# The recurrent gates as tanh of half the argument, in three rounded passes, with two steps of the recurrence on another engine

## The chip, the cores and the metric

The kernel runs on one core of a Trainium2 chip. The metric is the device time of one execution in microseconds (us). Five engines work at once, each through its own instructions in order: TensorE (PE, matmuls; PEld is its weight loading), VectorE (DVE), ScalarE (ACT), GpSimd (POOL) and SyncE (SP, which issues most DMAs). They wait for each other through semaphores only. All data is float32. An "fp32r" tile holds float32 numbers that were rounded, so that TensorE takes them in one pass.

## The reference, cut to what matters

Two transformer blocks run one after the other on 512 tokens of width 1024. The first (token mixer with a gated delta rule, then a mixture of 32 experts) is not touched by the change. The second has 16 meta tokens ahead of the 512, so T = 528. It runs attention and a two-way linear recurrence side by side, merges them and ends with a feed-forward layer. The change lies in the recurrence:

```python
xc = centred_dwconv(xr, conv_w[l], conv_b[l])            # 4 taps, xr = part of xn @ w_in
...
def rg_lru(xc, wa, ba, wx, bx, lam, reverse):            # once forward, once reverse
    xb = xf.reshape(B, T, RNN_BLOCKS, RNN_BLOCK)         # 8 blocks of 128 channels
    r = jax.nn.sigmoid(jnp.einsum('btnc,ncd->btnd', xb, wa) + ba)
    i = jax.nn.sigmoid(jnp.einsum('btnc,ncd->btnd', xb, wx) + bx)
    log_a = RG_C * r * jax.nn.log_sigmoid(lam)
    a = jnp.exp(log_a)
    u = jnp.sqrt(-jnp.expm1(2.0 * log_a)) * (i * xf)
    _, h = lax.associative_scan(_linear_recurrence_combine, (a, u), axis=1, reverse=reverse)
...
rnn = (forward + reverse) * jax.nn.gelu(gr)
mix = g_attn * attn + g_rnn * rnn
```

## The kernel before

The program is one straight stream per engine. The second block's mixing stage goes in eight rounds, n = 0 to 7: round n handles attention head n and recurrence block n, each 128 channels on the partitions and the tokens along the free axis. The order on PE is written out by hand (`manual_schedule` in `block2`); the order on the other engines is set by a scheduler when the program is built, except that ACT's table functions keep the order of the code (`act`). PSUM tiles come from three pools of two buffers each: `psA` and `psB` of one bank, `psD` of two banks. A tile is written again only when the reader of its old contents is done.

What PE does in a middle round, in its order, with the names used below:

- the gates (L2027): 2 directions x 2 gates, each one `psD` tile of two halves of 264 tokens; plain float32 matmuls of the weights `wg` with the convolved input `xc`. ACT empties each tile through a sigmoid into `rg` or `ig`.
- the scores of attention head n, token tiles 0 and 1, into `psD` (`weights`, through `mm3`, L198 to L200: high part, low part, high part again).
- two dense products (`dense_fm`, 24 passes of 512 columns each), the transposes of the first two score tiles between them, then the scores of token tiles 2 and 3.
- `rnn_x` of block n+1: a dense product of 2 x 24 passes of 264 columns into `psA`; ACT copies it to `xr`, DVE runs the four taps (L2007, L2009) into `xc`.
- the transposes of the last two score tiles, which ACT and DVE split into `PThi` and `PTlo`.
- the first dense product of round n+1, then the product of head n's weights with its values (`psB`, from `PThi` and `PTlo`), then the gates of round n+1. In round 7 two of the four gate tiles stand ahead of this product.

Behind the gates runs `rnn` for block n-1, without PE: tanh, exp and square on ACT, a product on DVE, two square roots on ACT (`th`), the products L2079 and one scan for each direction on DVE (L2082), their sum (L2084) and the product with the gate (L2085). `rn[n]` then goes into the mix (`ao`, L2144), which ACT and DVE split for the output product (`ga`, `rn`). Sigmoid, exp with tanh, and the square root lie in three different tables of ACT; every change between them is an ACT_TABLE_LOAD.

`split` is one ACT copy to the high part (L90) and one DVE subtraction for the low part (L170), so L90 and L170 stand for nearly all ACT work and all such subtractions.

Of the kernel before, what the change touches and what calls it, by code (L numbers as in the profile page):

```python
# [9 lines left out]
FT = mybir.dt.float32  # L10
FR = mybir.dt.float32r
I32 = mybir.dt.int32
BF = mybir.dt.bfloat16
AF = mybir.ActivationFunctionType
OP = mybir.AluOpType
# [18 lines left out]
META = 16  # L34
# [19 lines left out]
def halves(x):  # L54

    return x.rearrange("p (s c) -> p s c", s=2)


def by_turns(x):

    return x.rearrange("p (s c) -> p c s", s=2)


def unturned(x):

    return x.rearrange("p (c s) -> p s c", s=2)
# [9 lines left out]
class Net:  # L76
# [1893 lines left out]
    def rnn_start(self, p, vec):  # L1970

        nc = self.nc
        x = vec[:, 72:88]
        cl = p.tile([128, 2, 16], FT, name="cl")
        y = p.tile([128, 16], FT, name="cl_y")
        c = cl[:, 0, :]
        nc.vector.scalar_tensor_tensor(y, x, -1.0, x, op0=OP.mult, op1=OP.min)
        self.act(y, y, AF.Exp)
        self.log1p_unit(p, c, y, 16)
        nc.vector.tensor_scalar(y, x, 0.0, None, op0=OP.min)  # L1980
        nc.vector.tensor_tensor(c, y, c, OP.subtract)
        nc.vector.tensor_scalar(c, c, 8.0, None, op0=OP.mult)
        nc.vector.tensor_scalar(cl[:, 1, :], c, -1.0, None, op0=OP.mult)
        return cl

    def rnn_x(self, p, n, vec, xT):

        nc, I = self.nc, self.I
        T = META + S
        H = T // 2  # L1990
        nhi, nlo = xT
        wg = p.tile([128, 2, 2, 128], FT, name="wg")
        nc.sync.dma_start(wg[:, 0], I["rg_wa_2"][0, :, n].rearrange("d c e -> c d e"))
        nc.sync.dma_start(wg[:, 1], I["rg_wx_2"][0, :, n].rearrange("d c e -> c d e"))
        hi, lo = self.wchunk(I["w_in_2"][0], 0, NK, 1536 + n * 128, 128)
        xr = p.tile([128, T + 3], FT, name="xr")
        nc.vector.memset(xr[:, 0:2], 0.0)
        nc.vector.memset(xr[:, T + 2:], 0.0)
        for j in range(2):
            js = slice(j * H, (j + 1) * H)  # L2000
            ps = self.psA.tile([128, 512], FT, name="psA")
            for k in range(NK):
                self.mm3(ps[:, :H], hi[:, k, :], lo[:, k, :], by_turns(nhi[:, k, js]), by_turns(nlo[:, k, js]),
                         k == 0, k == NK - 1)
            self.act(halves(xr[:, 2 + j * H:2 + (j + 1) * H]), unturned(ps[:, :H]), AF.Copy)
        c = p.tile([128, T], FT, name="xc")
        nc.vector.tensor_scalar(c, xr[:, 0:T], vec[:, n:n + 1], vec[:, 32 + n:33 + n], op0=OP.mult, op1=OP.add)  # L2007
        for j in range(1, 4):
            nc.vector.scalar_tensor_tensor(c, xr[:, j:j + T], vec[:, 8 * j + n:8 * j + n + 1], c,  # L2009
                                           op0=OP.mult, op1=OP.add)  # L2010
        return c, wg

    def rnn_gates(self, p, n, vec, x, meanwhile=lambda: None):

        nc = self.nc
        T = META + S
        H = T // 2
        c, wg = x
        rg = p.tile([128, 2, T], FT, name="rg")
        ig = p.tile([128, 2, T], FT, name="ig")  # L2020
        for d in range(2):
            if d:
                meanwhile()
            for w, dst, bias in ((0, rg, 40), (1, ig, 56)):
                ps = self.psD.tile([128, 2, 512], FT, name="psD")
                for j in range(2):
                    nc.tensor.matmul(ps[:, j, :H], wg[:, w, d, :], c[:, j * H:(j + 1) * H], start=True, stop=True)  # L2027
                self.act(dst[:, d, :].rearrange("p (a b) -> p a b", a=2), ps[:, :, :H], AF.Sigmoid,
                         bias=vec[:, bias + 8 * d + n:bias + 8 * d + n + 1])
        nc.vector.tensor_tensor(ig, ig, c[:, None, :].to_broadcast([128, 2, T]), OP.mult)  # L2030
        return rg, ig

    def gates(self, p, n, xT, rn, ga):
# [25 lines left out]
    def rnn(self, p, n, cl, st, rn):  # L2059

        nc = self.nc
        T = META + S
        rg, ig = st
        u = p.tile([128, 2, T], FT, name="th", bufs=1)
        for d in range(2):
            q = 8 * d + n
            r, t = rg[:, d, :], u[:, d, :]
            self.act(t, r, AF.Tanh, scale=cl[:, 1, q:q + 1])
            self.act(r, r, AF.Exp, scale=cl[:, 0, q:q + 1])

            a2 = p.tile([128, T], FT, name="a2", bufs=1)
            self.act(a2, r, AF.Square)
            nc.vector.scalar_tensor_tensor(t, a2, 1.0, t, op0=OP.add, op1=OP.mult)
        yield
        for d in range(2):
            self.act(u[:, d, :], u[:, d, :], AF.Sqrt, scale=0.0625)
        for d in range(2):
            t, g, r = u[:, d, :], ig[:, d, :], rg[:, d, :]
            nc.vector.tensor_tensor(g, g, t, OP.mult)  # L2079
            if d:  # L2080
                t, g, r = t[:, ::-1], g[:, ::-1], r[:, ::-1]
            nc.vector.tensor_tensor_scan(t, r, g, 0.0, op0=OP.mult, op1=OP.add)  # L2082
        f = u[:, 0, META:]
        nc.vector.tensor_tensor(f, f, u[:, 1, META:], OP.add)  # L2084
        nc.vector.tensor_tensor(rn[n], rn[n], f, OP.mult)  # L2085
        yield

    def attention(self, tp, h, kv, rn, ga, gp, mix):
# [225 lines left out]
```

## Time and profile before

| | |
|---|---|
| time, median of 3 runs | 1925.61 us (1924.58 to 1929.8) |
| the profiled execution | 1932.37 us, span 1930.6 us |
| PE busy in the span | 1802.8 us (93%) |
| DVE, ACT, POOL busy | 987.3, 708.0, 31.1 us |
| the stretch of the eight rounds | about 1246 to 1563 us of the span |
| one middle round (gates to gates) | 34.70 us |

The profiled execution is the one the rows come from; it took 6.8 us longer than the median. The profile lists each instruction's start, its duration, and, in square brackets, the engine's idle time before it with what ended that. A PE row's duration contains the time that the pipeline takes to empty, so that rows overlap; how fast PE really goes is read from the distance between starts.

### The profile page before, as it was taken

The numbers are of one execution on the slowest core, as the hardware profiler recorded it, in microseconds if no ns is written. First come the engines' busy times: TensorE is split into PE (matmuls) and PEld (weight loads), VectorE is DVE, ScalarE is ACT, GpSimd is POOL, SyncE is SP. The second block draws the span as 40 slices with busy tenths as digits, with TensorE's granted clock in tenths as the row PEclk, the third lists the DMA queues.
The fourth block names the chain that finished last, engine by engine and source line by source line (L and its number), as shares of the span: only waits on it lengthen the run. The fifth ranks groups of instructions, "written<-read, shape, count | busy, mean of one in ns | idle before, by whom it ended". The sixth has DMA issues, their size and how long they took to land. (4 is left out here: it accounts for less than half of the span.)

```text
span 1930.6 us, 23857 instructions
## 1 busy us (share of the span) xinstructions
PE 1802.8 (93%) x9285; PEld 1357.0 (70%) x9285; DVE 987.3 (51%) x1843; ACT 708.0 (37%) x1157; POOL 31.1 (2%) x39
## 2 busy tenths in 40 slices
PE   6999999989999699988988968999999989999999
PEld 5887888868898534433333326888888778888887
DVE  6853787735555603222121249567877863333333
ACT  5333544424323311111010116457777733332332
POOL 0000000000000000000000000000000000000000
PEclk9999999989999799999999998999999999999999
DMA  8655766876286599999999873332222233333332
GB/s 256 98 121 94 126 88 88 152 173 97 77 298 260 223 425 424 425 426 425 425 425 426 369 274 134 115 109 67 71 77 66 87 100 104 104 98 102 103 123 66
DMA packets 252133, 372.65 MB, mean 193 GB/s; under 512 B 30386, under 2 KB 192723, under 8 KB 228083
## 3 DMA queue, kind: packets, MB, share of 16 engines
q1 hardware_dynamic: 241218, 342.79, 55.9%
q10 hardware_dynamic: 7632, 16.78, 2.3%
q0 software_dynamic: 3168, 11.54, 1.5%
q8 instruction: 74, 1.21, 0.3%
q14 instruction: 41, 0.33, 0.1%
HBM read 349.03 MB, written 22.04 MB: 192 GB/s over the span
## 5 line engine op out<-in xcount | busy, mean ns | idle before, releaser
L90 ACT ACTIVATE whi<-raw 128x1024 fp32r<-128x1024 f32 (+1 forms) x203 | 234.0, 1157 | 426.5 <-PE psA L199 267.2
L170 DVE TENSOR_TENSOR wlo<-raw,whi 128x1024 fp32r<-128x1024 f32 (+1 forms) x195 | 249.4, 1280 | 244.0 <-ACT whi L90 233.4
L1271 PE MATMUL psB<-mwt,XT 128*64 128x512 f32 x1008 | 234.2, 600 | 13.7 <-ACT XT L90 8.9
L1271 PEld LDWEIGHTS psB<-mwt,XT 128*64 128x64 f32 x1008 | 74.0, 138 | 161.4 <-issue 137.5
L200 PE MATMUL psA<-hT_hi,wlo 128*128 128x512 f32 (+1 forms) x456 | 176.4, 387 | 9.3 <-DVE wlo L170 9.3
L199 PE MATMUL psA<-hT_lo,whi 128*128 128x512 f32 (+1 forms) x456 | 177.6, 389 | 0.0
L198 PE MATMUL psA<-hT_hi,whi 128*128 128x512 f32 (+1 forms) x456 | 176.3, 387 | 0.9 <-ACT whi L90 0.9
L1304 PE MATMUL psB<-mwt,hbT 128*64 128x512 f32 x480 | 119.1, 604 | 23.1 <-DMA mwt<-in_w 21.8
L1336 DVE TENSOR_TENSOR res<-res,psA 128x512 f32<-128x512 f32 x128 | 79.4, 681 | 118.1 <-PE psA L1331 118.1
L199 PE MATMUL psA<-hn_lo,whi 128*128 128x512 f32 (+1 forms) x368 | 136.3, 370 | 0.3 <-DVE hn_lo L2178 0.3
L198 PE MATMUL psA<-hn_hi,whi 128*128 128x512 f32 (+1 forms) x368 | 136.4, 371 | 0.2 <-ACT hn_hi L90 0.2
L200 PE MATMUL psA<-hn_hi,wlo 128*128 128x512 f32 (+1 forms) x368 | 136.2, 370 | 0.0
L1280 DVE TENSOR_TENSOR sl<-sl,psB 128x512 f32<-128x512 f32 x16 | 11.0, 688 | 203.2 <-PE psB L1271 203.2
L198 PE MATMUL psA<-xn_hi,whi 128*128 128x512 f32 (+1 forms) x320 | 109.4, 342 | 0.4 <-ACT qx L90 0.4
L200 PE MATMUL psA<-xn_hi,wlo 128*128 128x512 f32 (+1 forms) x320 | 108.2, 338 | 0.0
L199 PE MATMUL psA<-xn_lo,whi 128*128 128x512 f32 (+1 forms) x320 | 108.1, 338 | 0.0
L1304 PEld LDWEIGHTS psB<-mwt,hbT 128*64 128x64 f32 x480 | 37.7, 138 | 98.6 <-issue 57.5
L200 PEld LDWEIGHTS psA<-hT_hi,wlo 128*128 128x128 f32 (+1 forms) x456 | 86.3, 189 | 22.0 <-DVE wlo L170 10.3
L90 ACT ACTIVATE hbT<-psA 128x512 f32<-128x512 f32 x16 | 9.6, 597 | 240.9 <-PE psA L1288 240.9
L198 PEld LDWEIGHTS psA<-hT_hi,whi 128*128 128x128 f32 (+1 forms) x456 | 86.3, 189 | 13.6 <-ACT whi L90 1.3
L199 PEld LDWEIGHTS psA<-hT_lo,whi 128*128 128x128 f32 (+1 forms) x456 | 86.3, 189 | 12.0
L199 PEld LDWEIGHTS psA<-hn_lo,whi 128*128 128x128 f32 x368 | 69.5, 189 | 9.5 <-DVE hn_lo L2178 0.5
(567 smaller groups left out, 3487.7 us busy)
## 6 DMA issues: line engine op xcount, KB each, us to landing
mwt<-in_w SPq DMA_DIRECT2D x188, 1024.0 KB, 20.6
raw<-in_w_in SPq DMA_DIRECT2D x108, 512.0 KB, 6.8
raw<-in_w_ffn_in SPq DMA_DIRECT2D x44, 512.0 KB, 3.9
raw<-in_w_ffn_out SPq DMA_DIRECT2D x22, 512.0 KB, 3.6
raw<-in_w_pa SPq DMA_DIRECT2D x8, 512.0 KB, 4.4
raw<-in_w_pb SPq DMA_DIRECT2D x8, 512.0 KB, 5.5
raw<-in_w_o SPq DMA_DIRECT2D x8, 512.0 KB, 7.7
raw<-in_w_out SPq DMA_DIRECT2D x8, 512.0 KB, 3.7
```

Source lines behind the costliest of these rows:

```text
L90: ins = self.nc.scalar.activation(out, in_, func, **kw)
L170: return self.nc.vector.tensor_tensor(lo, x, hi.bitcast(FT), OP.subtract)
L198: nc.tensor.matmul(out, whi, xhi, start=first, stop=False)
L199: nc.tensor.matmul(out, whi, xlo, start=False, stop=False)
L200: nc.tensor.matmul(out, wlo, xhi, start=False, stop=last)
L1271: nc.tensor.matmul(ps[CAP * i:CAP * (i + 1), :], XT[:, r0 + k, CAP * i:CAP * (i + 1)], w_, start=(r0 + k == 0), stop=(r0 + k == NK - 1))
L1280: nc.vector.tensor_tensor(so, so, h[1], OP.mult)
L1304: nc.tensor.matmul(pys[half][CAP * i:CAP * (i + 1), :], hT[:, r0 + k, CAP * i:CAP * (i + 1)], ws[i][:, k, half * 512:(half + 1) * 512], st ...
L1336: nc.vector.tensor_tensor(x, x, unturned(ps), OP.add)
```

## The change

- Gate weights `wg` and the convolved input `xc` are split into high and low parts (`ws`, `cs`), and each gate half is made by `mm3`: three passes of rounded operands in place of one float32 matmul. The input is read "by turns" (first and second half of the columns alternating), and ACT's reading of the tile undoes this.
- The sigmoid becomes tanh of half the argument. What follows is adapted: biases times one half, `c` times 4 in place of 8, `scale` and `bias` both given to the tanh and exp of `rnn`, `ig` made by (tanh + 1) times `xc`, another scale in the root.
- Behind the two roots a tanh of one column (`warm`) is put, so that the table with exp and tanh is loaded there.
- The last two steps of the recurrence (sum of directions, product with the gate) go from DVE to POOL.
- Buffers: `wghi`, `xclo` and `xc` have one buffer, the low weights share the name `wg` and the high input the name `xr`, with two buffers each.

```diff
-        nc.vector.tensor_scalar(c, c, 8.0, None, op0=OP.mult)
+        nc.vector.tensor_scalar(c, c, 4.0, None, op0=OP.mult)
+
+        nc.vector.tensor_scalar(vec[:, 40:72], vec[:, 40:72], 0.5, None, op0=OP.mult)
...
+        ws = p.tile([128, 2, 2, 128], FR, name="wghi", bufs=1), p.tile([128, 2, 2, 128], FR, name="wg")
+        self.split(*ws, wg)
...
-        c = p.tile([128, T], FT, name="xc")
+        c = p.tile([128, T], FT, name="xc", bufs=1)
...
-        return c, wg
+        cs = p.tile([128, T + 3], FR, name="xr")[:, 0:T], p.tile([128, T], FR, name="xclo", bufs=1)
+        self.split(*cs, c)
+        return c, cs, ws
...
-                    nc.tensor.matmul(ps[:, j, :H], wg[:, w, d, :], c[:, j * H:(j + 1) * H], start=True, stop=True)
-                self.act(dst[:, d, :].rearrange("p (a b) -> p a b", a=2), ps[:, :, :H], AF.Sigmoid,
+                    js = slice(j * H, (j + 1) * H)
+                    self.mm3(ps[:, j, :H], whi[:, w, d, :], wlo[:, w, d, :], by_turns(chi[:, js]), by_turns(clo[:, js]),
+                             True, True)
+                self.act(dst[:, d, :].rearrange("p (a s c) -> p a s c", a=2, s=2),
+                         ps[:, :, :H].rearrange("p a (c s) -> p a s c", s=2), AF.Tanh, scale=0.5,
                          bias=vec[:, bias + 8 * d + n:bias + 8 * d + n + 1])
-        nc.vector.tensor_tensor(ig, ig, c[:, None, :].to_broadcast([128, 2, T]), OP.mult)
+        nc.vector.scalar_tensor_tensor(ig, ig, 1.0, c[:, None, :].to_broadcast([128, 2, T]), op0=OP.add, op1=OP.mult)
...
-            self.act(t, r, AF.Tanh, scale=cl[:, 1, q:q + 1])
-            self.act(r, r, AF.Exp, scale=cl[:, 0, q:q + 1])
+            self.act(t, r, AF.Tanh, scale=cl[:, 1, q:q + 1], bias=cl[:, 1, q:q + 1])
+            self.act(r, r, AF.Exp, scale=cl[:, 0, q:q + 1], bias=cl[:, 0, q:q + 1])
...
-            self.act(u[:, d, :], u[:, d, :], AF.Sqrt, scale=0.0625)
+            self.act(u[:, d, :], u[:, d, :], AF.Sqrt, scale=0.25 ** 3)
+
+        self.act(self.small.tile([128, 1], FT, name="warm"), cl[:, 0, 0:1], AF.Tanh)
...
-        nc.vector.tensor_tensor(f, f, u[:, 1, META:], OP.add)
-        nc.vector.tensor_tensor(rn[n], rn[n], f, OP.mult)
+        nc.gpsimd.tensor_tensor(f, f, u[:, 1, META:], OP.add)
+        nc.gpsimd.tensor_tensor(rn[n], rn[n], f, OP.mult)
```

Where the instructions stand changes with it. On DVE, before, in a middle round, from the products of the roots (`ig<-ig,th`) on; the scans print as SCALAR_TENSOR_TENSOR `th<-rg,ig`:

```order
L2079 TENSOR_TENSOR ig<-ig,th 128x528 x2
L2007 TENSOR_SCALAR xc<-xr,vec_5912 128x528
L170 TENSOR_TENSOR PTlo<-psD,PThi 16x128
L2009 SCALAR_TENSOR_TENSOR xc<-xr,vec_5912,xc 128x528
L170 TENSOR_TENSOR PTlo<-psD,PThi 16x128
L2009 SCALAR_TENSOR_TENSOR xc<-xr,vec_5912,xc 128x528
L170 TENSOR_TENSOR PTlo<-psB,PThi 128x4x128
L2009 SCALAR_TENSOR_TENSOR xc<-xr,vec_5912,xc 128x528
L170 TENSOR_TENSOR PTlo<-psB,PThi 128x4x128
L2082 SCALAR_TENSOR_TENSOR th<-rg,ig 128x528 x2
L170 TENSOR_TENSOR wlo<-raw,whi 128x1024
L2084 TENSOR_TENSOR th<-th 128x512
```

And on DVE after, from the same place of a middle round on:

```order
L2090 TENSOR_TENSOR ig<-ig,th 128x528 x2
L2093 SCALAR_TENSOR_TENSOR th<-rg,ig 128x528 x2
L2011 TENSOR_SCALAR xc<-xr,vec_5912 128x528
L170 TENSOR_TENSOR PTlo<-psD,PThi 16x128
L2013 SCALAR_TENSOR_TENSOR xc<-xr,vec_5912,xc 128x528
L170 TENSOR_TENSOR PTlo<-psD,PThi 16x128
L2013 SCALAR_TENSOR_TENSOR xc<-xr,vec_5912,xc 128x528
L170 TENSOR_TENSOR PTlo<-psB,PThi 128x4x128
L2013 SCALAR_TENSOR_TENSOR xc<-xr,vec_5912,xc 128x528
L170 TENSOR_TENSOR PTlo<-psB,PThi 128x4x128
L2155 TENSOR_TENSOR ao<-ao,rn_8975 128x512
L170 TENSOR_TENSOR xclo<-xc,xr 128x528
```

The two scans moved ahead of the taps and of the four `PTlo`; the POOL steps can run from the second scan on, and the mix and the low part of the gates' input (`xclo`) follow the last `PTlo`. In round 7 the rows there are the same.

On ACT, before, in a middle round, from the splits of the next weights to the copies out of the gate tiles (`ga_10460<-ao` is the high part of a finished mix, `ga_8967<-psA` a merge gate):

```order
L90 ACTIVATE whi<-raw 128x1024 x2
L90 ACT_TABLE_LOAD
L90 ACTIVATE rg<-psD,vec_5912 128x528
L90 ACTIVATE ig<-psD,vec_5912 128x528
L90 ACTIVATE ga_10460<-ao 128x512
L90 ACTIVATE rg<-psD,vec_5912 128x528
L90 ACTIVATE ig<-psD,vec_5912 128x528
L90 ACTIVATE ga_8967<-psA 128x512
L90 ACT_TABLE_LOAD
L90 ACTIVATE pr,s<-psD,m,qs 128x528 x2
```

And on ACT after, from the same place on:

```order
L90 ACTIVATE whi<-raw 128x1024
L90 ACTIVATE xr<-xc 128x528
L90 ACTIVATE whi<-raw 128x1024
L90 ACTIVATE ga_10587<-ao 128x512
L90 ACTIVATE rg<-psD,vec_5912 128x528
L90 ACTIVATE ig<-psD,vec_5912 128x528
L90 ACTIVATE rg<-psD,vec_5912 128x528
L90 ACTIVATE wghi<-wg 128x512
L90 ACTIVATE ig<-psD,vec_5912 128x528
L90 ACTIVATE ga_8968<-psA 128x512
```

Both table loads are gone from this stretch, the mix's high part moved ahead of the four gate copies, and the high part of the next round's gate weights (`wghi`) stands ahead of the fourth. The table with exp is loaded directly behind the roots instead. After the last round the root of the following norm (`mo_r`) has a table load ahead of it that it had not before.

## Rows read from the trace of the kernel before

**Rows 1.** The page's first line.

```profile
span 1930.6 us, 23857 instructions
```

**Rows 2.** The windows view, one stretch of 35 us: busy time of each engine.

```profile
1365.00:1400.00 35.00, 33.93 (x198) 29.44 (x197) 28.07 (x52) 25.85 (x45) 0.00 (x0) 1.00 0.27 78
```

**Rows 3.** Timeline of PE, one middle round: start, duration, line, tiles, count, idle before.

```profile
1398.51 3.89 PE L2027 MATMUL psD<-xc,wg 128*128 128x264 f32 x16
1403.37 0.38 PE L198 MATMUL psD<-kThi,qhi 128*128 128x264 f32 x1 [0.96 <-ACT rg L90]
...
1404.82 0.38 PE L198 MATMUL psA<-xn_hi,whi 128*128 128x512 f32 x1
...
1416.56 0.28 PE L198 MATMUL psD<-kThi,qhi 128*128 128x264 f32 x1
...
1417.91 0.28 PE L198 MATMUL psA<-xn_hi,whi 128*128 128x264 f32 x1
...
1430.84 0.38 PE L199 MATMUL psB<-PTlo,v_hi 128*128 128x512 f32 x1
...
1433.21 3.89 PE L2027 MATMUL psD<-xc,wg 128*128 128x264 f32 x16
```

**Rows 4.** Timeline of ACT in the same round.

```profile
1402.09 0.63 ACT L90 ACTIVATE ga<-ao 128x512 fp32r<-128x512 f32 x1 [0.90 <-DVE xr L1998]
...
1406.57 1.28 ACT L90 ACT_TABLE_LOAD   x1 [2.18 <-DVE m L2108]
...
1423.70 1.18 ACT L90 ACTIVATE th<-th 128x528 f32<-128x528 f32 x2
```

**Rows 5.** Groups of ACT in all rounds: count, busy us, mean ns of one.

```profile
L90 ACT ACTIVATE th<-rg,cl 128x528 f32<-128x528 f32 x16 | 11.5, 720 | 0.0
...
L90 ACT ACTIVATE rg<-psD,vec 128x528 f32<-128x528 f32 x16 | 11.1, 694 | 7.2 <-PE psD L2027 7.0
...
L90 ACT ACTIVATE th<-th 128x528 f32<-128x528 f32 x16 | 9.4, 636 | 0.1
```

**Rows 6.** Timeline of DVE in the same round, from the products of the roots on.

```profile
1424.38 1.33 DVE L2079 TENSOR_TENSOR ig<-ig,th 128x528 f32<-128x528 f32 x2 [0.27 <-ACT th L90]
1425.62 0.55 DVE L2007 TENSOR_SCALAR xc<-xr,vec 128x528 f32<-128x528 f32 x1
1426.09 0.27 DVE L170 TENSOR_TENSOR PTlo<-psD,PThi 16x128 fp32r<-16x128 f32 x1
1426.29 0.75 DVE L2009 SCALAR_TENSOR_TENSOR xc<-xr,vec,xc 128x528 f32<-128x528 f32 x1
...
1429.12 0.67 DVE L170 TENSOR_TENSOR PTlo<-psB,PThi 128x512 fp32r<-128x512 f32 x1
1429.72 2.39 DVE L2082 TENSOR_TENSOR_SCAN th<-rg,ig 128x528 f32<-128x528 f32 x2
```

**Rows 7.** A POOL product, the DVE subtraction beside it, and all such subtractions (ns min/median/max).

```profile
346.29 2.38 POOL L659 TENSOR_TENSOR qk<-qk,Gb 128x1024 f32<-128x1024 f32 x1 [4.76 <-PE psB L649]
347.04 2.71 DVE L170 TENSOR_TENSOR wlo<-raw,whi 128x1024 fp32r<-128x1024 f32 x1
L170 DVE TENSOR_TENSOR wlo<-raw,whi x195: 293/1226/2708, 42.0 to 1918.0; 128x1024 fp32r<-128x1024 f32 x194, 128x128 fp32r<-128x128 f32 x1
```

**Rows 8.** Timeline of DVE and PE where round 7 begins.

```profile
1498.57 0.67 DVE L170 TENSOR_TENSOR PTlo<-psB,PThi 128x512 fp32r<-128x512 f32 x1
...
1498.98 1.94 PE L2027 MATMUL psD<-xc,wg 128*128 128x264 f32 x8
```

**Rows 9.** PE behind three long waits, and the window behind the last (PEclk is its seventh figure).

```profile
905.00 5.34 PE L1304 MATMUL psB<-mwt,hbT 128*64 128x512 f32 x14 [2.11 <-DMA mwt<-in_w]
967.40 3.65 PE L1304 MATMUL psB<-mwt,hbT 128*64 128x512 f32 x14 [2.21 <-DMA mwt<-in_w]
1555.40 0.80 PE L198 MATMUL psD<-whi,ga 128*128 128x512 f32 x1 [2.02 <-ACT ga L90]
1555.00:1560.00 5.00, 4.59 (x11) 3.69 (x12) 1.92 (x2) 2.36 (x3) 0.00 (x0) 0.50 0.93 319
```

More of the change, by code (lines that the diff above doesn't have):

```diff
@@ L2017, in rnn_gates @@
         H = T // 2
-        c, wg = x
+        c, (chi, clo), (whi, wlo) = x
         rg = p.tile([128, 2, T], FT, name="rg")
```

## The prediction

> **What bounds the kernel now.** I read the page's first line [rows 1] and then the windows of the mixing stage. In 35 us of a middle round PE is busy for 33.93, DVE for 28.07, ACT for 25.85 and POOL not at all, and PE's granted clock is 1.00 of full speed [rows 2]. So PE bounds this stage, and only two things can change the time: work that PE loses, and waits of PE. PE's timeline has one gates-to-gates period of 34.70 us (1398.51 to 1433.21) with one wait in it, 0.96 us ahead of the first score tile, ended by ACT's `rg` [rows 3]. That `rg` was late because ACT stood idle for 0.90 us and then did the mix's high part (0.63) first [rows 4]. All other engines have slack, but slack is not the same as being in time: the question for each of them is at which moment PE needs its result.
>
> **The gates.** From the gates' start to the first dense product is 1404.82 - 1398.51 = 6.31 us now [rows 3]. After, a gate tile is 2 halves x 3 passes of 264 columns. Twelve such passes of the score tiles take 1417.91 - 1416.56 = 1.35 us, 0.1125 each [rows 3], so a tile takes 0.675. PE is then faster than ACT, whose copy of a gate tile takes 0.694 [rows 5], and the chain goes by ACT: tile 1 written at 0.68, its copy done at 1.4, tile 3 (same buffer) written at 2.1 to 2.2, its copy done at 2.94. Then ACT does `wghi` (0.63, by the 128x512 activation of [rows 4]) and the fourth copy, done at about 4.25. The second score tile needs that buffer and ends 4.97 after the start. Gain: 6.31 - 4.97 = **1.34 us a round**. Rounds 2 to 6 get it, 6.7 us; round 7 has its gates in two parts and I give it 1.2. Rounds 0 and 1 I leave at 0: between their gates stand other loads of ACT, and the bound there is 1 either way.
>
> **ACT.** The sigmoid's table load goes and exp's moves behind the roots; a load takes 1.28, and the one shown was in PE's cover (ACT idle 2.18 before it) [rows 4]. Two splits (`xr<-xc`, 0.69; `wghi`) come in. Their cover is dense products of PE; without it they would cost what they last, but only `wghi` stands between two things that PE waits for, and it is counted above. The pointer biases of `th` and exp may cost what the copies with a bias pointer show over those without, 694 - 636 = 58 ns, at the highest 720 - 636 = 84 [rows 5]; four of them delay the roots by 0.2 to 0.3, the missing load brings them forward by more, and I take the products of the roots as starting when they do now, give or take 0.3 a round.
>
> **DVE: the order is the main thing.** The last full `PTlo` ends at 1429.12 + 0.67 = 1429.79 [rows 6]. PE reads it at 1430.84 [rows 3]. Slack: 1.05. The change puts the pair of scans, 2.39 us [rows 6], ahead of the taps and of all four `PTlo`. DVE has no idle time from the products on that could take them up (0.27 before the first [rows 6]). So `PTlo` ends 2.39 later, 1.33 us past its time, and PE waits that long in each product of weights and values. The shift of the gates doesn't help: everything in the round moves by the same amount.
>
> **POOL.** Two 128x512 products leave DVE and start as soon as the second scan ends, so exactly beside the taps and the `PTlo`. POOL took 2.38 for 128x1024 [rows 7]; half is 1.19 for each. What does DVE do meanwhile? One of the 195 weight subtractions ran beside a POOL product: it began at 347.04, POOL's began at 346.29 and ended at 348.67. The subtraction took 2.71 where the median is 1.226, and its end, 349.75, is POOL's end plus about one full duration (349.89) [rows 7]. It reads as DVE held until POOL was through. Applied here: each POOL step is 1.19, a small `PTlo` (0.27 [rows 6]; its one input from PSUM should let it pass) is all that proceeds under it, so each adds 1.19 - 0.27 = 0.92, both 1.84 (1.4 if the first tap, with a single tensor input, passes too; 0 if they don't hold one another). Wait of PE: 1.33 + 1.84 = **3.2 us**, in the products of heads of rounds 1 to 5: 5 x 3.2 = 16.0.
>
> The Trainium skill, "SBUF — State Buffer", section "Who interferes with whom", says that VectorE's second pair of ports is shared with GpSimd under an exclusive lock, held for a whole instruction, so that a VectorE operation with two SBUF inputs stands until the GpSimd one is done. This trace agrees with its 2.71 against 1.226 [rows 7]. By the rule the sum is the one below; if the 2.71 has another cause, it is the third case below.
>
> **Round 7.** There two gate tiles stand ahead of the product of head 6, and they need `xclo`. They start at 1498.98 now, and the last `PTlo` ends at 1498.57 + 0.67 = 1499.24 [rows 8]. After, they wait for that, the scans (2.39), the hold (1.84), the mix (`ao`, 0.67 as the 128x512 subtraction) and `xclo` itself (0.7): 1504.8, so +5.85; without the hold +4.0. In middle rounds `xclo` is ready before the gates, since these come behind the product that waits anyway.
>
> **The clock.** A wait of PE can cost more than itself. Behind a wait of 2.11 us 14 matmuls took 5.34; behind one of 2.21 the same took 3.65 [rows 9]: 1.69 lost the one time, nothing the other. Behind a wait of 2.02 the next 5 us had a granted clock of 0.50 with PE busy 4.59 [rows 9], which is the lower level (1.2 of 2.4 GHz) and up to 2.5 lost. Behind 0.96 in each round nothing was lost: the window has 1.00 [rows 2]. So 1.33 would likely be free and 3.2 not. I take (1.69 + 2.5) / 2 = 2.1 for each of six waits (five and round 7): 12.6, with 0 as the lower bound and 2.5 x 6 = 15 as the upper.
>
> **The end of the stage.** The last block's chain is scans, two steps, mix, high part, output product; PE waits 2.02 there now [rows 9]. The steps become 1.19 each instead of at most 0.67: +1.0. A table load ahead of the norm's root is new (1.28) and one earlier is gone. I take +2, between -1 (the loads' gain alone) and +4 (all of it, with two more small waits). The other edits (one scaling of a small vector, `8.0` to `4.0`, tanh in place of sigmoid, the added one in `ig`, which stays one instruction of two inputs like the 0.75 taps [rows 6]) go with what hides them now, 0; DVE's `ig` without its cover would be 0.1.
>
> **Sum.** -6.7 - 1.2 + 16.0 + 5.85 + 12.6 + 2 = **+28.5**. On the profiled execution (1932.37, the span of 1930.6 [rows 1] and 1.8 around it) that is 1961; on the median, 6.8 lower, **1954**.
>
> **The rivals.**
> - *Hold, but no fall of the clock.* For it: the 2.21 wait. Against: the other two. 28.5 - 12.6 = +15.9: 1941.5, with 1936 to 1947 for the bounds of the hold and the tail.
> - *No hold between POOL and DVE.* For it: the evidence is a single instruction, of another size. Waits are 5 x 1.33 = 6.7 and 4.0 in round 7, which alone may lose clock: 6.7 + 4.0 - 7.9 + 2 = +4.8, 1930, with 1923 to 1935. Near no change.
> - *Faster.* The one mechanism is that `PTlo` is in time in spite of the scans: the missing load brings `th` forward, ACT is done with the roots earlier, and the products and scans start that much before PE needs `PTlo`. It decides at 1.34: where the wait of the product stays below the gates' gain in each round, the gain wins. At a start 1.33 earlier and without the hold, no wait is left in the middle rounds and about 1 in round 7: -7.9 + 1 - 1 = -8, 1917.6. Against it: DVE's idle time before the products is 0.27 [rows 6], and what stands ahead of them on DVE is unchanged.
> - *The gates don't get shorter* (the copies of ACT then set their pace as before): all cases 7.9 higher, 1962 for the forecast; this is the upper end of the range.
>
> **How the numbers follow.** Forecast 0.43; hold without clock 0.20; no hold 0.18; faster 0.14; beyond 1965 (waits that grow into each other, or gates no shorter) 0.05. The measurement tells 0.3%, 5.8 us, from no change: 1919.8 to 1931.4. Faster takes the fourth case and the low end of the third, 0.15; same most of the third, 0.17; slower the rest, 0.68. The range leaves out the faster case and what is beyond: 1925 to 1965. The slower cases alone have 1936 to 1965.
>
> **What would show it.** Gates: 24 matmuls about 0.11 apart in place of 16 records, and the first dense product 5 us behind them. The product of weights: an idle time of about 3.2 on PE ahead of a matmul that reads `PTlo`, ended by DVE (1.3 without the hold; none in the faster case). Taps of over 1 us where a POOL product lies beside them, 0.75 without. Granted clock below 1.00 in the stretch behind these waits. Round 7's gates behind `xclo`. A period of about 34.7 - 1.3 + 3.2 + 2.1 = 38.7. I am wrong if DVE is through with `PTlo` in time, if POOL's steps don't touch DVE, or if the clock stays at 1.00 behind waits of 3 us.

## The result and the profile after

The changed kernel takes 1955.21 us (median of 4 runs, 1953.13 to 1960.54) where the kernel before took 1926.67 beside it: ratio 1.0151, 95% interval 1.0138 to 1.0165, so 28.5 us slower. The prediction was 1954.0 (1925 to 1965), slower. The page of the profiled execution begins:

```profile
span 1958.7 us, 24040 instructions
```

That is 28.1 us more than [rows 1]. All of it lies in the mixing stage and its end: from the first block's dense product to the first product of the feed-forward layer it is 334.7 us before and 364.1 after (1247.29 to 1582.00 and 1245.94 to 1610.05 by PE's starts). The windows of three middle rounds:

```profile
1351.00:1386.00 35.00, 31.91 (x187) 27.78 (x187) 28.36 (x50) 22.81 (x42) 3.02 (x2) 0.95 0.22 64
1386.00:1421.00 35.00, 31.90 (x192) 28.03 (x191) 26.31 (x47) 22.69 (x41) 3.02 (x2) 0.95 0.25 73
1421.00:1456.00 35.00, 31.78 (x178) 27.34 (x177) 27.77 (x47) 22.98 (x41) 3.02 (x2) 0.90 0.23 68
```

Against [rows 2], PE lost 2 us of busy time in 35, the granted clock is 0.95 to 0.90 where it was 1.00, and POOL appears with 3.02 us in two instructions. PE's timeline of one round, from the product of weights and values to the first dense product:

```profile
1403.96 0.48 PE L198 MATMUL psB<-PThi,v_hi 16*128 16x512 f32 x1 [2.70 <-DVE PTlo L170]
...
1409.16 0.28 PE L198 MATMUL psD<-xr,wghi 128*128 128x264 f32 x1
...
1413.63 0.38 PE L198 MATMUL psD<-kThi,qhi 128*128 128x264 f32 x1 [0.17 <-ACT ig L90]
...
1414.41 0.38 PE L198 MATMUL psA<-xn_hi,whi 128*128 128x512 f32 x1
```

Three things answer to [rows 3]. The product now waits 2.70 us for DVE's `PTlo` (2.69 to 2.81 in all five rounds). It then lasts 1409.16 - 1403.96 = 5.20 to the first gate, where it took 1433.21 - 1429.68 = 3.53 before. And the gates' start to the first dense product is 5.25 in place of 6.31. DVE and POOL in front of such a wait, the one that ends at 1442.04:

```profile
1435.14 2.40 DVE L2093 TENSOR_TENSOR_SCAN th<-rg,ig 128x528 f32<-128x528 f32 x2
1437.46 0.53 DVE L2011 TENSOR_SCALAR xc<-xr,vec 128x528 f32<-128x528 f32 x1
1437.91 0.27 DVE L170 TENSOR_TENSOR PTlo<-psD,PThi 16x128 fp32r<-16x128 f32 x1
1438.11 1.59 DVE L2013 SCALAR_TENSOR_TENSOR xc<-xr,vec,xc 128x528 f32<-128x528 f32 x1
1439.62 0.27 DVE L170 TENSOR_TENSOR PTlo<-psD,PThi 16x128 fp32r<-16x128 f32 x1
1439.82 1.56 DVE L2013 SCALAR_TENSOR_TENSOR xc<-xr,vec,xc 128x528 f32<-128x528 f32 x1
1441.31 0.68 DVE L170 TENSOR_TENSOR PTlo<-psB,PThi 128x512 fp32r<-128x512 f32 x1
1441.91 0.75 DVE L2013 SCALAR_TENSOR_TENSOR xc<-xr,vec,xc 128x528 f32<-128x528 f32 x1
...
1437.71 1.42 POOL L2095 TENSOR_TENSOR th<-th 128x512 f32<-128x512 f32 x1 [34.98 <-DVE th L2093]
1439.21 1.61 POOL L2096 TENSOR_TENSOR rn<-rn,th 128x512 f32<-128x512 f32 x1
```

The two taps that begin beside a POOL product last 1.59 and 1.56; the one that begins after POOL's end takes 0.75, as in [rows 6]. The first `PTlo` of a full tile ends at 1441.31 + 0.68 = 1441.99, and PE starts at 1442.04.

In round 7 the gates wait, first for `xr` (the high part of their input, which stands behind the last tap) and then for `xclo`; at the end of the stage PE waits for a high part of the output weights. The rows of PE:

```profile
1520.88 0.59 PE L198 MATMUL psD<-xr,wghi 128*128 128x264 f32 x1 [4.05 <-ACT xr L90]
1522.02 0.59 PE L199 MATMUL psD<-xclo,wghi 128*128 128x264 f32 x1 [0.55 <-DVE xclo L170]
...
1575.34 0.72 PE L198 MATMUL psD<-whi,ga 128*128 128x512 f32 x1 [3.87 <-ACT whi L90]
```

The wait at the end is reached through POOL. There POOL's first step lies beside low parts of weights on DVE and lasts 3.81; ACT, whose next tanh overwrites what POOL still reads, stands idle behind it, and the high parts of the weights stand behind that tanh. POOL and ACT:

```profile
1560.93 3.81 POOL L2095 TENSOR_TENSOR th<-th 128x512 f32<-128x512 f32 x1 [42.62 <-DVE th L2093]
...
1566.13 0.83 ACT L90 ACTIVATE th<-rg,cl 128x528 f32<-128x528 f32 x1 [3.36 <-POOL rn L2096]
```

### The profile page after: what moved, and what is told of

It is laid out like the page before. It is cut to its first block, busy times and chain, and to the rows that moved or that the text cites. A ratio compares the mean times of both kernels' runs of the same rounds, so it can differ in the third digit from the quotient of the medians.

```text
span 1958.7 us, 24040 instructions
## 1 busy us (share of the span) xinstructions
PE 1810.5 (92%) x9349; PEld 1365.8 (70%) x9349; DVE 996.1 (51%) x1844; ACT 711.1 (36%) x1174; POOL 56.8 (3%) x55
## 5 line engine op out<-in xcount | busy, mean ns | idle before, releaser
L1304 PE MATMUL psB<-mwt,hbT 128*64 128x512 f32 x480 | 119.1, 604 | 22.8 <-DMA mwt<-in_w 21.5
```

The source lines that it names most:

```text
L1304: nc.tensor.matmul(pys[half][CAP * i:CAP * (i + 1), :], hT[:, r0 + k, CAP * i:CAP * (i + 1)], ws[i][:, k, half * 512:(half + 1) * 512], st ...
```

## The experiments

The theory was that of the prediction: the scans ahead of `PTlo`, lengthened by POOL holding DVE, make PE wait, and the waits lower the clock. The rivals: that the order alone makes the wait, that POOL costs wherever it is, that the gates in three passes give nothing, and that the slow passes have another cause than the wait. "Stage" below is the length from the first block's dense product to the feed-forward layer in the profiled execution, 334.7 us before and 364.1 after.

**The two steps back on DVE.**

```diff
-        nc.gpsimd.tensor_tensor(f, f, u[:, 1, META:], OP.add)
-        nc.gpsimd.tensor_tensor(rn[n], rn[n], f, OP.mult)
+        nc.vector.tensor_tensor(f, f, u[:, 1, META:], OP.add)
+        nc.vector.tensor_tensor(rn[n], rn[n], f, OP.mult)
```

> The changed kernel with the two last steps of the recurrence back on DVE; on DVE the scans still stand ahead of the taps and of the four PTlo, in the same order up to the last PTlo. If a POOL product holds DVE (my theory): the two taps that lasted 1.59 and 1.56 us beside POOL go back to 0.75, the third PTlo ends 1.65 us earlier, PE's wait ahead of the product of weights and values falls from 2.7 to about 1.1 us and the clock behind it does not fall; 5 rounds x 3.7 and some 6 us in round 7 and behind it go, about 1930 us (1924 to 1936). If the order alone made the wait (rival): wait still about 2.7 us, time about 1955.

Measured: 1939.56 us, ratio 1.0071 (1.0054 to 1.0088), stage 346.0. DVE's order up to the last `PTlo` is that of the changed kernel. Its taps, from the second on, and PE:

```profile
1424.04 0.75 DVE L2013 SCALAR_TENSOR_TENSOR xc<-xr,vec,xc 128x528 f32<-128x528 f32 x1
...
1424.92 0.75 DVE L2013 SCALAR_TENSOR_TENSOR xc<-xr,vec,xc 128x528 f32<-128x528 f32 x1
...
1426.32 0.48 PE L198 MATMUL psB<-PThi,v_hi 16*128 16x512 f32 x1 [1.16 <-DVE PTlo L170]
```

The taps are back at 0.75 and the wait is 1.04 to 1.16. So the 2.70 are about 1.05 from the order and 1.65 from POOL beside DVE. The time is 3.6 us above the expected range, since two things stayed that were expected to go. Round 7 still waits 2.40 for `xr` and 0.76 for `xclo`, and the product behind that lasts 6.43. And the clock does fall behind waits this short: the five products last 3.76, 5.43, 3.76, 5.25 and 5.18. Their windows (PEclk is the seventh figure; where the clock stayed, the window reaches into the gates):

```profile
1318.80:1324.10 5.30, 5.21 (x27) 4.16 (x27) 5.30 (x9) 1.99 (x3) 0.00 (x0) 1.00 0.00 0
1354.20:1359.90 5.70, 5.62 (x17) 4.26 (x18) 5.70 (x9) 2.22 (x3) 0.00 (x0) 0.70 0.03 8
1390.60:1395.90 5.30, 5.25 (x27) 4.16 (x27) 5.30 (x8) 2.03 (x3) 0.00 (x0) 1.00 0.00 0
1426.30:1432.00 5.70, 5.68 (x19) 4.38 (x20) 5.70 (x8) 2.22 (x3) 0.00 (x0) 0.70 0.02 6
1462.50:1468.00 5.50, 5.49 (x17) 4.12 (x18) 5.50 (x8) 2.23 (x3) 0.00 (x0) 0.71 0.01 3
```

Three of five lost clock, behind waits of 1.04, 1.16 and 1.04; two behind 1.04 did not. I had taken 1.33 to be free because 0.96 was [rows 2, 3].

**Scans behind the last `PTlo`, with the steps on POOL and on DVE.** `lastPT` is the last `PTlo` of the round.

```diff
-            nc.vector.tensor_tensor_scan(t, r, g, 0.0, op0=OP.mult, op1=OP.add)
+            s = nc.vector.tensor_tensor_scan(t, r, g, 0.0, op0=OP.mult, op1=OP.add)
+            if n < NK - 1:
+                self.after(s, self.lastPT)
```

> The changed kernel with the scans of rounds 1 to 7 made to follow the last PTlo; the two steps stay on POOL, and POOL's products then lie beside the low parts of weights. If only the order against PTlo matters (my theory): PE does not wait for PTlo, the gates' gain of about 1.1 us a round is left, about 1920 us (1915 to 1926). If products on POOL cost wherever they lie (rival), since the low parts of the weights come late: 1930 to 1945.

> Both of these: scans behind the last PTlo and the two steps on DVE, so that of the change the three-pass gates, tanh and the table load behind the roots are left. Theory: no wait for PTlo, clock 1.00 in all middle rounds, about 1919 us (1915 to 1923), faster than the kernel before. Rival (the gates in three passes give nothing, since the copies of ACT set their pace): about 1926.

Measured: 1951.17 us with POOL (ratio 1.0127, 1.011 to 1.0144) and 1937.84 without (1.0056, 1.004 to 1.0073). Both expectations failed, theory and rival alike. PE no longer waits for `PTlo`, but it waits at the score tiles: 3.91 us for `rg` with POOL, 2.05 for `ig` without. ACT and PE of the run without POOL:

```profile
1362.32 0.70 ACT L90 ACTIVATE rg<-psD,vec 128x528 f32<-128x528 f32 x1 [0.36 <-PE psD L200]
1364.79 0.63 ACT L90 ACTIVATE ga<-ao 128x512 fp32r<-128x512 f32 x1 [1.77 <-DVE xr L2002]
1365.33 0.68 ACT L90 ACTIVATE ig<-psD,vec 128x528 f32<-128x528 f32 x1
...
1366.06 0.38 PE L198 MATMUL psD<-kThi,qhi 128*128 128x264 f32 x1 [2.05 <-ACT ig L90]
```

The mix's high part `ga<-ao` stands ahead of the fourth copy and needs `ao`, which comes last in the chain scans, two steps, mix. (The row names a memset of `xr`; that stood behind the mix on DVE, which ended at 1364.76 where ACT starts at 1364.79.) Later scans make this place wait. It is the wait of 0.96 in [rows 3, 4] again, grown.

**Only POOL.** In the kernel before, the two steps move to POOL, nothing else.

> The kernel before with only the two steps moved to POOL; its order on DVE keeps the scans behind the last PTlo. Theory: DVE's low parts of the weights are held by up to 2 us but nothing that PE needs at once, so about 1928 us (1924 to 1934). Rival (the two steps on POOL alone make the loss): 1945 to 1955.

Measured: 1963.33 us, ratio 1.0186 (1.0169 to 1.0204), stage 370.0. The rival was right that this part alone makes a loss; it is above the rival's range, and larger than that of the whole change. ACT, POOL, DVE and PE:

```profile
1371.30 0.63 ACT L90 ACTIVATE ga<-ao 128x512 fp32r<-128x512 f32 x1 [6.86 <-DVE xr L1998]
1371.95 1.28 ACT L90 ACT_TABLE_LOAD   x1
1373.25 0.70 ACT L90 ACTIVATE rg<-psD,vec 128x528 f32<-128x528 f32 x1
...
1366.00 3.21 POOL L2084 TENSOR_TENSOR th<-th 128x512 f32<-128x512 f32 x1 [36.35 <-DVE th L2082]
1369.29 1.26 POOL L2085 TENSOR_TENSOR rn<-rn,th 128x512 f32<-128x512 f32 x1
...
1365.75 2.32 DVE L170 TENSOR_TENSOR wlo<-raw,whi 128x1024 fp32r<-128x1024 f32 x2
...
1374.00 3.89 PE L2027 MATMUL psD<-xc,wg 128*128 128x264 f32 x8 [5.02 <-ACT rg L90]
```

Here it is POOL that stands: its first product starts 0.25 behind the first of two subtractions on DVE, which keep their 1.16 each, and takes 3.21, where the second takes 1.26 beside an idle DVE. The mix is then late, `ga<-ao` with it, and behind that the table load and the first copy: PE waits 5.02 in the middle of the gates.

**The mix's high part behind the fourth copy**, in three kernels: with scans behind and steps on DVE (there `wghi` too goes behind the fourth copy), in the kernel before with the steps on POOL, and in the kernel before alone. `lastG` is the last copy out of a gate tile.

```diff
-        self.split(*mix[h], o)
+        self.after(self.act(mix[h][0], o, AF.Copy), self.lastG)
+        nc.vector.tensor_tensor(mix[h][1], o, mix[h][0].bitcast(FT), OP.subtract)
```

> Scans behind the last PTlo, the two steps on DVE, and on ACT the high part of the mix and that of the next gate weights behind the fourth copy out of the gate tiles. If what is left of the loss is this place of the mix's high part (theory): no wait of PE at the second score tile (2.05 us in the run with scans and steps put back), first dense product about 4.3 us after the gates' start in place of 6.3, round 7 waits about 2.5 us for xclo: about 1916 us (1911 to 1923). If the fourth copy is late for another reason (rival): wait stays near 2 us and time near 1937.

> The kernel before with the two steps on POOL and, on ACT, the mix's high part behind the fourth copy out of the gate tiles. If moving the steps alone cost 36 us because the copy of the first gate tile stood behind the mix's high part, which waits for POOL (theory): the wait of 5.0 us goes, about 1921 us (1917 to 1928). If POOL beside DVE costs by itself (rival): over 1940 still.

> The kernel before with only the mix's high part behind the fourth copy out of the gate tiles. Theory: the wait of 0.96 us a round goes, 6 x 0.96 = 5.8, about 1921 us (1918 to 1925). Rival (the table load ahead of the first copy or PE's float32 gates set the pace anyway): 1926.

Measured: 1922.04 us (ratio 0.9985, 0.9975 to 0.9994; stage 327.3), 1929.3 (1.0022, 1.0009 to 1.0035; stage 336.9) and 1924.51 (0.9994, 0.9985 to 1.0004; stage 332.8). This one place in ACT's queue takes 34 us off the POOL kernel (32 if each run is set against the kernel before beside it). Its POOL product still takes 3.22 and the mix still comes as late, but nothing that PE needs stands behind it; some 5 us against the kernel with the steps on DVE remain, a little above what I expected. Of these, 3.2 lie at the end of the stage, from the start of the last product of weights to the feed-forward layer: 53.1 against 49.9. In all three the waits for copies are gone, and a smaller one shows in their place, 0.2 to 0.7 us of the transposes for the softmax products on DVE, and they eat nearly all that the third gained: its middle round takes 34.54 us (34.70 before). Its time can't be told from that of the kernel before, since the interval holds 1, so that its theory (about 1921) is not confirmed and its rival (1926) not excluded. A middle round of the first takes 33.3 us.

**PE kept busy through the wait.** In the changed kernel, 12 more passes into the tile of the dense product ahead of it; the real product overwrites them, so this run does more work.

```diff
+        for k in range(extra):
+            self.nc.tensor.matmul(ps, hi[:, k % NK, :], by_turns(xhi[:, k % NK, :]), start=k == 0, stop=k == extra - 1)
```

> The changed kernel with 12 more passes of 512 columns (2.6 us) ahead of the dense product before the product of weights and values in rounds 2 to 6; their result is overwritten. They fill the wait of 2.7 us with work. If the wait lowers the granted clock (theory): the passes of the product stay 0.216 us apart, clock 1.00 there, five times 1.5 to 3 us come back, about 1945 us (1940 to 1949). If the passes are slow for another reason, such as what DVE and POOL do to the memory (rival): 0.43 apart as before, about 1955.

Measured: 1946.74 us, ratio 1.0116 (1.0099 to 1.0133), with 60 passes more (stage 353.2). That is 21.5 us above the kernel before beside it, where the changed kernel was 28.5 above: 7 us less (8.5 by the two medians alone). The windows of two products in the changed kernel, and then the same two of this run:

```profile
1326.60:1333.30 6.70, 6.61 (x15) 4.88 (x16) 5.40 (x8) 2.11 (x3) 0.00 (x0) 0.51 0.25 72
1365.90:1371.50 5.60, 5.58 (x17) 4.18 (x18) 5.34 (x7) 2.11 (x3) 0.00 (x0) 0.70 0.11 29
```

```profile
1320.60:1324.20 3.60, 3.58 (x15) 2.71 (x16) 3.60 (x6) 2.22 (x3) 0.00 (x0) 1.00 0.00 0
1356.90:1360.50 3.60, 3.52 (x14) 2.66 (x15) 3.60 (x7) 2.22 (x3) 0.00 (x0) 1.00 0.02 5
```

With DVE and ACT just as busy beside it, the product takes 3.6 to 3.75 and the granted clock is 1.00. The slow passes came from the wait ahead of them, not from the neighbours.

**Copies on POOL.** The first run (steps on DVE), with two POOL copies of the second scan's result where the steps had been; nobody reads them.

```diff
+        for _ in range(2):
+            nc.gpsimd.tensor_copy(a2[:, :S], u[:, 1, META:])
```

> The run with the two steps back on DVE, and beside it, on POOL, two copies of 128x512 from the result of the second scan into a tile that nobody reads; the order on DVE is the same. If any POOL instruction that reads and writes SBUF holds DVE's taps (theory, the lock): taps beside a copy last over 1 us again, PE's wait ahead of the product of weights and values grows from 1.04 to 1.5 to 2.7 us, about 1945 to 1955. If only products with two inputs on POOL hold them (rival): taps 0.75, wait 1.04, about 1940.

Measured: 1943.28 us (one run), stage 352.8. DVE's taps and POOL:

```profile
1427.91 0.92 DVE L2013 SCALAR_TENSOR_TENSOR xc<-xr,vec,xc 128x528 f32<-128x528 f32 x1
...
1428.95 0.91 DVE L2013 SCALAR_TENSOR_TENSOR xc<-xr,vec,xc 128x528 f32<-128x528 f32 x1
...
1427.50 0.77 POOL L2096 COPY a<-th 128x512 f32<-128x512 f32 x1 [35.27 <-DVE th L2093]
1428.33 0.97 POOL L2096 COPY a<-th 128x512 f32<-128x512 f32 x1
```

Between the two expectations: a copy with one input holds the taps too, but it lasts 0.77 to 0.97 and not 1.4 to 1.6, so only 0.17 is added to each tap, and PE's wait grows to 1.37 to 1.48. The hold is not a matter of products. In this run the taps end at 1428.83 and 1429.86, the copies at 1428.27 and 1429.30; in the changed kernel the taps end at 1439.70 and 1441.38, POOL's steps at 1439.13 and 1440.82 (sums of the rows shown). Each of the four taps ends 0.56 or 0.57 behind the POOL instruction beside it. That the smaller hold is the same mechanism is read from these ends, not shown otherwise.

**Further order.** The kernel with scans behind and steps on DVE once more, with another order around it: scans behind `xclo` as well; the high parts of the mix and of `wg` behind the second exp of the round; the gating product behind the maxima; the low parts of the mix and of `wg` behind the softmax products.

> Scans behind the last PTlo and behind xclo, the two steps on DVE; on ACT the mix's high part behind the second exp of the round, on DVE the gating product and the low parts of the mix and of the gate weights behind the maxima or the softmax products. Theory: the wait of 0.5 to 0.67 us of the transposes for the softmax products goes, in round 7 the gates' wait of 1.31 us for xclo goes: about 4.5 us below the run before it, near 1917 us (1913 to 1921). Rival (PE's waits there are set by the maxima's own chain of DVE and ACT, 0.5 us whatever stands around it): about 1922.

Measured: 1921.25 us against 1927.21 beside it, ratio 0.9964 (0.9952 to 0.9977), stage 325.1. It beats both kernels; the 1917 of the theory was not reached, since only one of its two waits went. The windows of two middle rounds:

```profile
1351.00:1386.00 35.00, 34.77 (x214) 31.10 (x213) 30.45 (x59) 27.78 (x53) 0.00 (x0) 1.00 0.29 86
1386.00:1421.00 35.00, 34.77 (x213) 30.90 (x213) 30.18 (x57) 27.51 (x49) 0.00 (x0) 1.00 0.24 69
```

The middle rounds show no wait of PE now (33.0 us each). Round 7's wait of 1.30 for `xclo` stayed: with the scans out of the way, DVE does a low part of weights (1.20 us) ahead of it. The stage is 9.6 us shorter than before in the profiled executions and the medians differ by 6.0; for the kernel of 1922.04 us the figures are 7.4 and 3.2. Where the 3 to 4 us lie is open: the kernel before has one profiled execution, and it is 6.8 us above its median.

## Why the prediction was right

**Gates.** Predicted 1.34 a round, measured 1.06: the chain by ACT's copies is as written, with about 0.1 more at each change of engine. Another 0.29 a round came from a place that the prediction did not name: the transposes of the first two score tiles take 1.01 to the next dense product, where they took 1.30. What shortened them was not tested.

**The wait ahead of the product.** Predicted 3.2 (order 1.33, hold 1.84), measured 2.7 (1.05 and 1.65). The place was wrong in a detail: PE stops at the product's first pass, which reads `PThi`, and not at the first that reads the late `PTlo`. It starts as the third `PTlo` ends. By the code that is the reader of the `psB` buffer (two in all) which the product is written to. In the kernel before, the third `PTlo` and the product's first pass are these:

```profile
1427.84 0.67 DVE L170 TENSOR_TENSOR PTlo<-psB,PThi 128x512 fp32r<-128x512 f32 x1
...
1429.68 0.48 PE L198 MATMUL psB<-PThi,v_hi 16*128 16x512 f32 x1
```

So the slack was 1429.68 - 1428.51 = 1.17 and not 1.05. The last `PTlo` costs another 0.2 inside the product: in the run with PE kept busy, at full clock, the first pass that reads it starts at 1321.89, behind its end at 1321.84, and the product takes 3.75 in place of 3.53.

**The hold.** Taps 1.59 beside a POOL product, 0.92 beside a copy, 0.75 alone: the reading of the one overlapped subtraction [rows 7] carried over to another operation and size. The small `PTlo`, which has one of its inputs in PSUM, keeps its 0.27 beside POOL, as predicted. The Trainium skill, "SBUF — State Buffer", section "Who interferes with whom", adds that the order of issue decides which of the two engines stands. The runs agree: DVE stands in the changed kernel, and POOL stands (3.21 in place of 1.26) where DVE was first.

**Round 7.** Predicted 5.85, measured 4.05 + 0.55 = 4.6 of idle time. Part of the difference lies in the counting: the first gate pass needs only the high part and runs between the two waits. The first pass that reads `xclo` starts 1522.02 - 1516.83 = 5.2 behind the end of the dense product, so the term was too large by some 0.7, of which 0.2 is the shorter hold.

**The clock.** Predicted 2.1 for each wait. The five products last 6.65, 5.45, 5.20, 6.60 and 5.44 in place of 3.53, 11.7 more, of which some 0.2 each also stand in the run at full clock: 2.1 each. In round 7 it was more: the two gate tiles ahead of the product ran at the low level too, and the product lasts 6.61. The window of both:

```profile
1520.90:1531.30 10.40, 9.85 (x27) 7.60 (x28) 3.94 (x5) 2.79 (x4) 0.00 (x0) 0.51 0.33 101
```

An estimate from it is 9.85 x (1 - 0.51) = 4.8 lost there. That waits of 1.33 would be free was wrong, as the run with the steps on DVE showed.

**The end.** Predicted +2, measured +2.1 from the last product of weights to the feed-forward layer, but by another way, so that the match is luck. The norm's new table load shows in PE's wait by 0.2 at most (0.50 in place of 0.28). What costs is POOL: in the five kernels with the steps on POOL this stretch takes 52.6 to 53.5 us, in the six that leave POOL out, the kernel before among them, 49.7 to 50.5, and with the copies that nobody reads 52.1. In the trace a POOL step that DVE stretched to 3.81 leads to it, with ACT behind POOL and the weights' high parts behind ACT. ACT stood idle for this step before too (3.04, now 3.36), so how the longer step becomes 2.1 us of PE is not shown.

**The sum.** That 28.5 was met to a tenth is luck as well: the waits ahead of the five products (16.0 and 13.6) and round 7 came out smaller than predicted, the loss of clock larger (12.6 against 2.1 x 5 and 4.8, some 15), and these errors cancel.

**What I had not seen** is that the parts don't add. POOL alone costs 36 us; with the scans moved forward, as the change has them, the mix is in time again for ACT's queue and the loss moves to `PTlo`. I costed the scans' move as the harm and POOL as its addition. In fact moving the scans back cures one wait and opens another; both went only when ACT's order was changed too, in the run with the steps on DVE.

## What to carry to other kernels

An instruction that frees nothing for the busiest engine, like the mix's high part here, belongs behind those that do, on every engine's queue: two lines of order were worth 32 to 34 us of POOL's 36. Moving work to an idle POOL is not free for DVE even if DVE has slack, since here either stood until the other's instruction was through; look at what lies beside it. And price a wait of PE with its clock: waits of 1 to 3 us cost up to three more in these runs.

## What had not been expected of the hardware

A wait of 1.04 to 1.16 us before a product was followed by a mean granted clock of 0.70 or 0.71 over that product in three rounds of five, while 0.96 in the kernel before, at another place of the round, left the clock at 1.00. Filling 2.7 us of wait in five rounds with passes that nobody reads made the changed kernel some 7 us faster. And a POOL product of 128x512 takes 1.26 beside an idle DVE, 1.4 to 1.6 beside taps on DVE, and 3.2 to 3.8 when DVE came first.
